# One 512-column subtraction on VectorE in place of two of 256, and a new list of order moves

## The chip, the core and the metric

The kernel runs on one core of a Trainium2 chip. The core has five engines that run side by side: TensorE (PE in the profile: matmuls; its weight loads are PEld), VectorE (DVE), ScalarE (ACT), GpSimd (POOL) and SyncE (SP), which here issues most of the DMAs that bring weights from HBM. They work on tiles of 128 partitions in SBUF; matmuls write to PSUM, in eight banks of 512 float32 columns. The metric is the device time of one execution in microseconds (us), lower is better. The kernel before took 1205.26 us, the median of three runs (1204.7, 1205.26, 1209.56).

## The reference

A decoder trunk of two layers, with 512 tokens and a model width of 1024, in float32. Layer 0 mixes causal pooling with an attention that keeps the 128 best-scored keys of each query; layer 1 is a gated linear recurrence. Each mixer is followed by a gated feed-forward network. Every block begins with an RMS norm and adds its result to `x`:

```python
def rmsnorm(x, g):
    xf = x.astype(jnp.float32)
    y = xf * lax.rsqrt(jnp.mean(xf * xf, axis=-1, keepdims=True) + EPS)
    return (y * g.astype(jnp.float32)).astype(x.dtype)

def swiglu(h, w_gate_up, w_down):
    gu = h @ w_gate_up
    gate, up = gu[..., :D_FF], gu[..., D_FF:]
    return (jax.nn.silu(gate) * up) @ w_down

for layer in range(DEPTH):
    h = rmsnorm(x, ln_mix[layer])
    ...                                   # layer 0: pooling and attention; layer 1: recurrence
    x = x + mixed @ w_out
    h = rmsnorm(x, ln_ffn[layer])
    x = x + swiglu(h, w_gate_up[layer], w_down[layer])
return rmsnorm(x, ln_final)
```

## The kernel before

**Data.** The residual `x` lies transposed in eight tiles `xT`, 128 model rows by 512 tokens each. A float32 product is made of three matmuls: weight and operand are each split into a high part, rounded to a faster float32 form, and a low correction. `wh`, `wl` are the two parts of 512 (or 384) weight columns; `BH[i]`, `BL[i]` those of an operand. ScalarE makes the high part by a copy, VectorE (for some GpSimd) subtracts it from the source to get the low one. Both `wh` and `wl` are rings of six buffers. Raw weights come into three buffers `raw`.

**Seven products for eight.** The input projections of the feed-forward networks and of layer 1 use a Strassen-like scheme on 2 by 2 blocks. The operand's halves by tokens are called here block one (tokens 0 to 255, z = 0) and block two (256 to 511, z = 1). For each i of 0 to 3, of model rows i and i + 4, the operand tiles `BH[i]` and `BL[i]` hold seven slots of 256 columns: B11, B21 (rows i and i + 4 of block one), B22 (row i + 4 of block two), and four sums. With y11, y21 the block-one rows and y12, y22 the block-two rows:

- T1 = y11 - y12, T3 = y22 - y12, T2 = y22 - T1, T4 = y21 - T2.

`pairs` (L837) first runs the products that need only B11 and B21 (`first`, `second`: 5 weight slabs before layer 1, 10 before a feed-forward network), which gives TensorE work while the sums are made. Then `rest` (L760) goes through S1 with T1, S2 with T2, S3 with T3, S4 with B22 and A22 with T4 for each slab.

**The bridges.** `Bridge` (L608) stands between two blocks. `add` and `add_half` add a product to `xT`, square it, and at the last tile of a token half run `norm` (column sums with the matrix `ones`, a square root, and a broadcast by matmuls with `idn`). `build` (L653) then makes the operands of that half. Three bridges use this `build`: r0 (before the feed-forward network of layer 0, around 205 us of the profile), r1 (before layer 1, around 560 us) and r2 (before the last feed-forward network, around 845 us). For z = 1 the kernel before has, per i, t3 on GpSimd and t1 on VectorE, each 256 columns, then t2 and t4 on VectorE. T1 and T2 lie in one page (`ta`), T3 and T4 in another (`tb`), so that one copy and one subtraction split a page. The low part of page `tb` is made by GpSimd for i = 1 and 3.

**Pages.** Temporary tiles of 512 columns come from a pool, first in, first out (18 pages from the first feed-forward network on). Who takes a page must wait until its last reader has finished.

**Order.** Nothing runs in the order of the code. `Plan` records every instruction with its operands and an estimated cost; `issue` (L400) schedules them by a list scheduler, and then applies each entry of `MOVES` (a seed, a strength, a start and a width of a stretch): it shakes the priorities in that stretch and keeps the order if the estimated end is earlier. The instructions are then issued in that order on each engine, and an engine's queue is strictly in order. All of them show one line in the profile (L425 before).

Of the kernel before, what the change touches and what calls it, by code (L numbers as in the profile page):

```python
# [15 lines left out]
ALU = mybir.AluOpType  # L16
AX = mybir.AxisListType

P = 128
T = 512  # L20
H2 = T // 2
# [19 lines left out]
ITERS = 6  # L41

MOVES = (
# [31 lines left out]
)  # L75
PAGES = 38
RPAGES = 20
# [10 lines left out]
TWO_PI_3 = float(np.float32(2 * np.pi - 6.28125 - 0.001953125))  # L88
MAGIC = 12582912.0

B11, B21, B22, T1, T2, T3, T4 = range(7)
OPND = {"A11": B11, "A12": B21, "A22": T4, "S2": T2, "S3": T3, "S1": T1, "S4": B22}

class Op:
# [334 lines left out]
def trunk(ctx: ExitStack, tc: tile.TileContext, xt, xp, pos, vecs, ident, dup, tri, lmask, invc, select,  # L429
          w_ab, w_kw, w_pool, w_oa, w_ob, w_c, w_oc, w_gu, w_dn, w_dq, out):  # L430
    nc = Plan(tc)
# [3 lines left out]
    def new(shape, dt, name):  # L435
        t = cp.tile(shape, dt, name=name)
        return t[tuple(slice(None) for _ in shape)]
# [33 lines left out]
    pages = Pool([new([P, T], F32, f"pg{i}") for i in range(PAGES - RPAGES)] + early_pg[NR:])  # L471
# [136 lines left out]
    class Bridge:  # L608
# [44 lines left out]
        def build(self, z, ts, rp):  # L653
            for i in range(4):
                bh, bl = BH[i], BL[i]
                pg = pages.get()
                ya, yb = pg[:, :H2], pg[:, H2:]
                for j, y in ((i, ya), (i + 4, yb)):
                    nc.vector.scalar_tensor_tensor(y, xT[j][:, ts], vec[:, self.gcol + j:self.gcol + j + 1], rp, ALU.mult, ALU.mult)
                if z == 0:  # L660
                    self.y[i] = pg
                    for s, y, e in ((B11, ya, nc.gpsimd), (B21, yb, nc.vector)):
                        h = bh[:, s * H2:(s + 1) * H2]
                        nc.scalar.activation(h, y, AF.Copy)
                        e.tensor_tensor(bl[:, s * H2:(s + 1) * H2], y, f32(h), ALU.subtract)
                else:
                    y11, y21 = self.y[i][:, :H2], self.y[i][:, H2:]
                    ta, tb = pages.get(), pages.get()
                    t1, t2, t3, t4 = ta[:, :H2], ta[:, H2:], tb[:, :H2], tb[:, H2:]
                    h = bh[:, B22 * H2:(B22 + 1) * H2]  # L670
                    nc.scalar.activation(h, yb, AF.Copy)
                    nc.gpsimd.tensor_sub(t3, yb, ya)
                    nc.vector.tensor_sub(t1, y11, ya)
                    nc.vector.scalar_tensor_tensor(t2, t1, -1.0, yb, ALU.mult, ALU.subtract)
                    nc.vector.scalar_tensor_tensor(t4, t2, -1.0, y21, ALU.mult, ALU.subtract)
                    h3, h1 = bh[:, 5 * H2:], bh[:, 3 * H2:5 * H2]
                    nc.scalar.activation(h3, tb, AF.Copy)
                    nc.scalar.activation(h1, ta, AF.Copy)
                    nc.vector.tensor_tensor(bl[:, B22 * H2:(B22 + 1) * H2], yb, f32(h), ALU.subtract)
                    (nc.gpsimd if i % 2 else nc.vector).tensor_tensor(bl[:, 5 * H2:], tb, f32(h3), ALU.subtract)  # L680
                    nc.vector.tensor_tensor(bl[:, 3 * H2:5 * H2], ta, f32(h1), ALU.subtract)
                    pages.put(self.y[i], ta, tb, pg)


    class Stage:
# [965 lines left out]
```

## Time and profile before

| | us |
|---|---|
| median of 3 runs | 1205.26 |
| the profiled execution | 1208.27 |
| span in its trace, first to last instruction | 1206.5 |
| PE busy | 1175.2 |
| DVE busy | 974.0 |
| ACT busy | 755.9 |
| POOL busy | 225.4 |

The profiled execution is 3.0 us longer than the median. PE is busy 97% of the span and DVE 81%. Busy shares are means over stages that differ: the rows further down show single stretches. The chain of work that ended last goes through PE for 76% of the span.

### The profile page before, as it was taken

How to read it: one execution, taken by the hardware profiler on the slowest of the kernel's cores; microseconds unless marked ns; L12 is line 12 of the kernel's file. 1: busy time of each engine (PE TensorE's matmuls, PEld its weight loads, DVE VectorE, ACT ScalarE, POOL GpSimd, SP SyncE). 2: the span in 40 equal slices, each digit the busy share in tenths (PEclk: the TensorE clock that was granted, in tenths of full speed). 3: DMA queues.
4: the chain of work that ended last, by engine and by line, in shares of the span. 5: the costliest groups of instructions: out<-in, count | busy, mean ns of one | idle time of the engine just before them, and what ended most of it. 6: DMA issues, size and time to landing. Idle time of an engine off the chain costs nothing.

```text
span 1206.5 us, 23123 instructions
## 1 busy us (share of the span) xinstructions
PE 1175.2 (97%) x8562; PEld 1077.9 (89%) x8563; DVE 974.0 (81%) x2116; ACT 755.9 (63%) x1753; POOL 225.4 (19%) x209
## 2 busy tenths in 40 slices
PE   8998999999999999998999999999999999999996
PEld 6776658999999988998999999988999999998996
DVE  7799966987777794778999999976987777795676
ACT  6336965766666762656877767744766566673563
POOL 4465012221101001102222211111221111000111
PEclk9997999999999999998999999999999999999999
DMA  8221113599877535467674445216599876634652
GB/s 314 102 70 53 36 39 84 187 235 237 233 182 190 127 110 148 130 160 202 196 190 118 125 119 143 71 53 158 163 233 243 219 183 167 169 97 129 150 151 70
DMA packets 72369, 180.60 MB, mean 150 GB/s; under 512 B 6144, under 2 KB 20544, under 8 KB 72256
## 3 DMA queue, kind: packets, MB, share of 16 engines
q1 hardware_dynamic: 51584, 141.37, 36.3%
q0 software_dynamic: 20672, 37.75, 18.9%
q8 instruction: 67, 1.10, 0.4%
q14 instruction: 46, 0.38, 0.1%
HBM read 177.00 MB, written 2.10 MB: 148 GB/s over the span
## 4 chain that ended last, share of the span: by engine, by line
PE 76%; DVE 6%; DMA 5%; ACT 2%; issue 1%; POOL 0%; DVEq 0%; ACTq 0%; POOLq 0%
PE bk L425 76%; DMA raw<-in_w_dq 3%; DVE wl L425 2%; DVE pg L425 2%; DMA raw<-in_w_gu 2%; ACT wh L425 1%; ACT pg L425 1%; DVE xT L425 1%; DVE raw L425 0%; DVE BL L425 0%; ACT bk L425 0%; ACT BH L425 0%; DVE sm L425 0%; DVE pr L425 0%; POOL pg L425 0%
## 5 line engine op out<-in xcount | busy, mean ns | idle before, releaser
L425 PE MATMUL bk<-BH,wh 128*128 128x256 f32 (+1 forms) x2088 | 581.7, 297 | 12.5 <-ACT wh L425 3.5
L425 PE MATMUL bk<-BL,wh 128*128 128x256 f32 (+1 forms) x2088 | 584.7, 294 | 0.0
L425 PE MATMUL bk<-BH,wl 128*128 128x256 f32 (+1 forms) x2088 | 576.6, 295 | 1.1 <-DVE wl L425 1.1
L425 ACT ACTIVATE wh<-raw 128x512 fp32r<-128x512 f32 (+2 forms) x644 | 378.4, 602 | 280.1 <-PE bk L425 229.0
L425 DVE TENSOR_TENSOR wl<-raw,wh 128x512 fp32r<-128x512 f32 (+1 forms) x609 | 397.0, 670 | 119.2 <-ACT wh L425 97.3
L425 PEld LDWEIGHTS bk<-BH,wh 128*128 128x128 f32 x2088 | 388.3, 192 | 29.4 <-ACT bk L425 6.3
L425 PEld LDWEIGHTS bk<-BL,wh 128*128 128x128 f32 x2088 | 391.6, 192 | 8.0 <-issue 0.8
L425 PEld LDWEIGHTS bk<-BH,wl 128*128 128x128 f32 x2088 | 387.4, 192 | 10.3 <-DVE wl L425 1.9
L425 PE MATMUL bk<-pr,wh 128*128 128x256 f32 (+1 forms) x784 | 190.3, 331 | 0.0
L425 PEld LDWEIGHTS bk<-pr,wh 128*128 128x128 f32 x784 | 132.1, 188 | 14.8 <-ACT wh L425 0.2
L425 PE MATMUL bk<-pr,wl 128*128 128x256 f32 (+1 forms) x392 | 128.6, 333 | 0.6 <-DVE wl L425 0.6
L425 DVE TENSOR_TENSOR raw<-raw 128x512 f32<-128x512 f32 (+1 forms) x152 | 100.8, 668 | 14.9 <-DMA raw<-in_w_gu 8.6
L425 POOL DMA_DIRECT2D raw<-in_w_gu x44 | 47.9, 1089 | 334.7 <-DVE wl L425 135.7
L425 DVE TENSOR_TENSOR pg<-pg,pg 128x256 f32<-128x256 f32 (+2 forms) x203 | 100.0, 504 | 8.8 <-ACT pg L425 4.0
L425 ACT COPY pg<-bk 128x256 f32<-128x256 f32 (+6 forms) x212 | 76.4, 365 | 33.8 <-PE bk L425 28.8
L425 ACT COPY bk<-bk 128x256 f32<-128x256 f32 x222 | 77.6, 362 | 20.5 <-PE bk L425 20.3
L425 PEld LDWEIGHTS bk<-pr,wl 128*128 128x128 f32 x392 | 73.4, 188 | 8.0 <-DVE wl L425 1.3
L425 PE MATMUL bk<-pg,pg 128*128 128x128 f32 (+3 forms) x578 | 69.0, 260 | 1.0 <-DVE pg L425 0.7
L425 PEld LDWEIGHTS bk<-pg,pg 128*128 128x128 f32 (+3 forms) x578 | 56.3, 167 | 8.1 <-ACT pg L425 2.1
L425 POOL TENSOR_TENSOR wl<-raw,wh 128x512 fp32r<-128x512 f32 (+3 forms) x35 | 45.5, 1303 | 94.2 <-ACT wh L425 86.9
L425 POOL TENSOR_TENSOR pg<-pg,pg 128x256 f32<-128x256 f32 (+1 forms) x36 | 38.1, 1058 | 132.1 <-ACT pg L425 59.0
L425 POOL DMA_DIRECT2D raw<-in_w_dq x16 | 17.5, 1102 | 216.3 <-DVE wl L425 103.9
(167 smaller groups left out, 1068.1 us busy)
## 6 DMA issues: line engine op xcount, KB each, us to landing
raw<-in_w_gu SPq DMA_DIRECT2D x44, 768.0 KB, 6.3
raw<-in_w_gu SPq DMA_DIRECT2D x64, 512.0 KB, 5.5
raw<-in_w_gu POOLq DMA_DIRECT2D x44, 512.0 KB, 6.3
raw<-in_w_c SPq DMA_DIRECT2D x16, 768.0 KB, 5.6
raw<-in_w_c SPq DMA_DIRECT2D x21, 512.0 KB, 4.2
raw<-in_w_dq SPq DMA_DIRECT2D x16, 576.0 KB, 5.4
raw<-in_w_c POOLq DMA_DIRECT2D x16, 512.0 KB, 5.6
raw<-in_w_dn SPq DMA_DIRECT2D x16, 448.0 KB, 3.4
```

The costliest lines, as they stand in the source:

```text
L425: getattr(self.real[o.eng], o.call)(*map(_real, o.args), **{k: _real(v) for k, v in o.kw.items()})
```

## The change

Block one now takes two pages per i, and each row of block two is written into the free half of one of them: page `pa` holds y11 and y22, page `pb` y12 and y21. Then `pa` less y12 taken twice is T1 and T3 in one VectorE instruction of 512 columns. The slots are renumbered so that T1 and T3 share a page and T2 and T4 the other. GpSimd's subtraction and VectorE's of 256 columns are gone. GpSimd still makes the low part of page `tb` for i = 1 and 3, which is now the one of T2 and T4. Each i takes four pages as before, two of them earlier. `MOVES` is another list, of 73 entries (92 before), so the order of instructions is new over the whole program.

```diff
 MOVES = (
-    (353236198, 1000, 372111, 20000), (664781755, 200, 1057486, 200000), (787263731, 2000, 158073, 40000),
+    (4522707, 2000, 934044, 40000), (491263128, 1000, 214385, 40000), (889732538, 2000, 362822, 40000),
...
-B11, B21, B22, T1, T2, T3, T4 = range(7)
+B11, B21, B22, T1, T3, T2, T4 = range(7)
...
-                pg = pages.get()
-                ya, yb = pg[:, :H2], pg[:, H2:]
+                if z == 0:
+                    self.y[i] = pages.get(), pages.get()
+                pa, pb = self.y[i]
+
+                ya, yb = (pa[:, :H2], pb[:, H2:]) if z == 0 else (pb[:, :H2], pa[:, H2:])
...
-                    t1, t2, t3, t4 = ta[:, :H2], ta[:, H2:], tb[:, :H2], tb[:, H2:]
+                    t1, t3, t2, t4 = ta[:, :H2], ta[:, H2:], tb[:, :H2], tb[:, H2:]
                     h = bh[:, B22 * H2:(B22 + 1) * H2]
                     nc.scalar.activation(h, yb, AF.Copy)
-                    nc.gpsimd.tensor_sub(t3, yb, ya)
-                    nc.vector.tensor_sub(t1, y11, ya)
+                    two = lambda x: x.rearrange("p (a b) -> p a b", a=2)
+                    nc.vector.tensor_tensor(two(ta), two(pa), ya[:, None, :].to_broadcast([P, 2, H2]), ALU.subtract)
                     nc.vector.scalar_tensor_tensor(t2, t1, -1.0, yb, ALU.mult, ALU.subtract)
...
-                    pages.put(self.y[i], ta, tb, pg)
+                    pages.put(pa, pb, ta, tb)
```

**VectorE at r1, block two.** Before, from the first row of block two on; `bk_150` is the broadcast norm of block two, `pg_141` the page of T1 and T2, `pg_127` that of T3 and T4, both of i = 0:

```order
L425 SCALAR_TENSOR_TENSOR pg_133<-xT_65,vec,bk_150 128x256
L425 SCALAR_TENSOR_TENSOR pg_133<-xT_69,vec,bk_150 128x256
L425 TENSOR_TENSOR pg_141<-pg_134,pg_133 128x256
L425 SCALAR_TENSOR_TENSOR pg_130<-xT_70,vec,bk_150 128x256
L425 SCALAR_TENSOR_TENSOR pg_141<-pg_141,pg_133 128x256
L425 TENSOR_TENSOR wl_92<-raw_81,wh_86 128x512
L425 TENSOR_TENSOR wl_95<-raw_81,wh_89 128x512
L425 SCALAR_TENSOR_TENSOR pg_127<-pg_141,pg_134 128x256
L425 SCALAR_TENSOR_TENSOR pg_130<-xT_66,vec,bk_150 128x256
L425 TENSOR_TENSOR wl_94<-raw_82,wh_88 128x512
L425 TENSOR_TENSOR BL_77<-pg_127,BH_73 128x512
```

Now, from the same row on; `pg_142` and `pg_132` are the two pages of i = 0, `pg_139` is T1 and T3, `pg_133` T2 and T4:

```order
L419 SCALAR_TENSOR_TENSOR pg_132<-xT_65,vec,bk_150 128x256
L419 SCALAR_TENSOR_TENSOR pg_142<-xT_69,vec,bk_150 128x256
L419 SCALAR_TENSOR_TENSOR pg_138<-xT_66,vec,bk_150 128x256
L419 TENSOR_TENSOR pg_139<-pg_142,pg_132 128x512
L419 SCALAR_TENSOR_TENSOR pg_135<-xT_70,vec,bk_150 128x256
L419 SCALAR_TENSOR_TENSOR pg_133<-pg_139,pg_142 128x256
L419 TENSOR_TENSOR pg_130<-pg_135,pg_138 128x512
L419 TENSOR_TENSOR BL_77<-pg_139,BH_73 128x512
L419 SCALAR_TENSOR_TENSOR pg_133<-pg_133,pg_132 128x256
```

The subtraction is 512 wide, the first page that is split is that of T1 and T3, and the corrections of weights that stood among these rows stand elsewhere.

**PE just before r1.** The last product of the layer 0 network into bank `bk_143` is nine rows of `BH`, three of `BL` and six matmuls with `pr`, 18 in all, and the column sums with `ones` belong to the two norms (`bk_150` block one, `bk_149` block two). Before, the 18 stand ahead of all of these rows:

```order
L425 MATMUL bk_143<-pr_3414,wl_93 128x256
L425 MATMUL bk_150<-ones,pg_125 128x1
L425 MATMUL bk_150<-ones,pg_128 128x1
...
L425 MATMUL bk_149<-ones,pg_137 128x1
L425 MATMUL bk_148<-idn,sm_98 128x128 x2
L425 MATMUL bk_146<-BH_73,wh_88 128x256
```

Now they stand between the two norms:

```order
L419 MATMUL bk_150<-ones,pg_126 128x1
L419 MATMUL bk_143<-BH_73,wh_86 128x256
L419 MATMUL bk_143<-BL_77,wh_86 128x256
...
L419 MATMUL bk_143<-pr_3475,wl_93 128x256
L419 MATMUL bk_149<-ones,pg_125 128x1
L419 MATMUL bk_148<-idn,sm_98 128x128 x2
```

The sums of block one no longer wait in PE's queue for the 18 matmuls.

**GpSimd at r1.** Before, `pg_127`, `pg_129`, `pg_136` and `pg_137` are written with T3, between the corrections of the operands:

```order
L425 TENSOR_TENSOR BL_79<-pg_140,BH_75 128x256
L425 TENSOR_TENSOR pg_127<-pg_133 128x256
L425 TENSOR_TENSOR pg_129<-pg_130 128x256
L425 TENSOR_TENSOR BL_78<-pg_129,BH_74 128x512
L425 TENSOR_TENSOR pg_136<-pg_142 128x256
L425 TENSOR_TENSOR pg_137<-pg_128 128x256
L425 TENSOR_TENSOR BL_80<-pg_137,BH_76 128x512
```

Now these four rows are gone, and the two corrections of 512 columns are of T2 and T4:

```order
L419 TENSOR_TENSOR BL_79<-pg_131,BH_75 128x256
L419 TENSOR_TENSOR BL_80<-pg_127,BH_76 128x256
L419 TENSOR_TENSOR BL_78<-pg_136,BH_74 128x512
L419 TENSOR_TENSOR BL_80<-pg_141,BH_76 128x512
L419 DMA raw_82<-in_w_c 128x2x512
```

GpSimd has 12 instructions less in the whole program, four at each bridge.

## Rows read from the trace of the kernel before

**Rows 1.** The page's first part: busy us, share of span, count.
```profile
PE 1175.2 (97%) x8562; PEld 1077.9 (89%) x8563; DVE 974.0 (81%) x2116; ACT 755.9 (63%) x1753; POOL 225.4 (19%) x209
```

**Rows 2.** Stretches at r0, r1, r2: stretch, length, busy by engine, clock, DMA share, GB/s.
```profile
215.00:245.00 30.00, 29.87 (x247) 29.48 (x246) 29.13 (x53) 24.65 (x57) 8.66 (x7) 1.00 0.64 193
...
555.00:590.00 35.00, 30.56 (x215) 29.55 (x215) 34.10 (x72) 24.47 (x57) 11.46 (x12) 0.85 0.65 188
...
849.00:880.00 31.00, 30.50 (x252) 30.11 (x252) 30.32 (x54) 24.52 (x56) 7.03 (x6) 1.00 0.57 185
```

**Rows 3.** Timeline of PE at r1: start, us, instruction, count, [idle before, releaser].
```profile
555.79 1.22 PE L425 MATMUL bk<-idn,sm 128*128 128x128 f32 x4 [0.32 <-DVE sm L425]
558.04 0.58 PE L425 MATMUL bk<-BH,wh 128*128 128x256 f32 x1 [1.03 <-ACT BH L425]
...
560.83 0.41 PE L425 MATMUL bk<-BH,wh 128*128 128x256 f32 x1
561.04 0.46 PE L425 MATMUL bk<-BL,wh 128*128 128x256 f32 x1
...
566.22 0.58 PE L425 MATMUL bk<-BH,wh 128*128 128x256 f32 x1 [2.58 <-ACT pg L425]
...
581.28 0.38 PE L425 MATMUL bk<-idb 128*128 128x512 bf16 x1
...
586.23 0.50 PE L425 MATMUL bk<-BH,wh 128*128 128x256 f32 x2 [0.51 <-ACT bk L425]
```

**Rows 4.** Timeline of ACT at r1.
```profile
565.79 0.37 ACT L425 COPY pg<-bk 128x256 f32<-128x256 f32 x1 [1.49 <-DVE BL L425]
```

**Rows 5.** Timeline of DVE at r1.
```profile
554.50 0.16 DVE L425 TENSOR_SCALAR sm<-bk 128x2 f32<-128x2 f32 x1 [0.36 <-PE bk L425]
...
557.06 0.48 DVE L425 SCALAR_TENSOR_TENSOR pg<-xT,vec,bk 128x256 f32<-128x256 f32 x1
...
557.99 2.44 DVE L425 SCALAR_TENSOR_TENSOR pg<-xT,vec,bk 128x256 f32<-128x256 f32 x6
560.34 0.82 DVE L425 TENSOR_TENSOR pg<-pg,pg 128x256 f32<-128x256 f32 x1
...
564.49 1.21 DVE L425 TENSOR_TENSOR BL<-pg,BH 128x512 fp32r<-128x512 f32 x1
...
574.97 1.45 DVE L425 TENSOR_TENSOR pg<-pg,pg 128x256 f32<-128x256 f32 x2
...
585.77 1.89 DVE L425 TENSOR_TENSOR wl<-raw,wh 128x512 fp32r<-128x512 f32 x3
587.57 1.09 DVE L425 TENSOR_TENSOR BL<-pg,BH 128x256 fp32r<-128x256 f32 x3
```

**Rows 6.** Timeline of POOL at r1.
```profile
560.84 0.92 POOL L425 TENSOR_TENSOR pg<-pg 128x256 f32<-128x256 f32 x1
564.05 1.11 POOL L425 TENSOR_TENSOR pg<-pg 128x256 f32<-128x256 f32 x1 [2.29 <-DVE pg L425]
...
574.14 2.00 POOL L425 TENSOR_TENSOR pg<-pg 128x256 f32<-128x256 f32 x2 [4.28 <-DVE pg L425]
582.41 1.68 POOL L425 TENSOR_TENSOR BL<-pg,BH 128x512 fp32r<-128x512 f32 x1 [6.27 <-ACT BH L425]
```

**Rows 7.** Groups by form: shapes, count, busy us, mean ns, idle before.
```profile
L425 POOL TENSOR_TENSOR pg<-pg 128x256 f32<-128x256 f32 x10 | 10.3, 1034 | 28.2 <-DVE pg L425 28.2
...
L425 POOL TENSOR_TENSOR BL<-pg,BH 128x512 fp32r<-128x512 f32 x5 | 8.2, 1633 | 20.6 <-ACT BH L425 17.3 <-DVE pg L425 3.3
...
L425 DVE TENSOR_TENSOR pg<-bk,idn 128x512 f32<-128x512 f32 x8 | 5.4, 679 | 0.0
```

**Rows 8.** Timeline of DVE, PE and POOL at r2.
```profile
851.43 1.23 DVE L425 TENSOR_TENSOR wl<-raw,wh 128x512 fp32r<-128x512 f32 x1
...
852.73 0.39 PE L425 MATMUL bk<-BH,wl 128*128 128x256 f32 x1 [0.34 <-DVE wl L425]
...
851.33 0.79 POOL L425 TENSOR_TENSOR pg<-pg 128x256 f32<-128x256 f32 x1 [4.43 <-DVE pg L425]
```

More of the change, by code (lines that the diff above doesn't have):

```diff
@@ L660, in build @@
                 if z == 0:
-                    self.y[i] = pg
                     for s, y, e in ((B11, ya, nc.gpsimd), (B21, yb, nc.vector)):
@@ L666, in build @@
                 else:
-                    y11, y21 = self.y[i][:, :H2], self.y[i][:, H2:]
+                    y21 = pb[:, H2:]
                     ta, tb = pages.get(), pages.get()
-                    t1, t2, t3, t4 = ta[:, :H2], ta[:, H2:], tb[:, :H2], tb[:, H2:]
+                    t1, t3, t2, t4 = ta[:, :H2], ta[:, H2:], tb[:, :H2], tb[:, H2:]
                     h = bh[:, B22 * H2:(B22 + 1) * H2]
                     nc.scalar.activation(h, yb, AF.Copy)
-                    nc.gpsimd.tensor_sub(t3, yb, ya)
-                    nc.vector.tensor_sub(t1, y11, ya)
+                    two = lambda x: x.rearrange("p (a b) -> p a b", a=2)
+                    nc.vector.tensor_tensor(two(ta), two(pa), ya[:, None, :].to_broadcast([P, 2, H2]), ALU.subtract)
                     nc.vector.scalar_tensor_tensor(t2, t1, -1.0, yb, ALU.mult, ALU.subtract)
```

54 rows, old and new, of the table MOVES are left out of this document.

## The prediction

> **What bounds the kernel now.** I read the page's first part first, because it says how much any change could win: PE is busy 1175.2 us of a span of 1206.5, so it stands idle 31.3 us in the whole program [rows 1]. The change takes no matmul away. What it can give is a part of these 31.3 us, or of time that PE runs at its lower clock. The windows around the three bridges come second, to see which engine leads in each [rows 2]. At r0 PE is busy 29.87 of 30 us and at r2 30.50 of 31, both at a granted clock of 1.00, while DVE is busy 29.13 and 30.32: DVE is nearly full there, but PE does not wait for it. At r1 it does: PE is busy 30.56 of 35 us, the clock is 0.85, and DVE is busy 34.10. So r1 is the place to take apart, and PE's timeline there comes third [rows 3]. Its marked waits are 0.32, 1.03, 2.58 and 0.51 us, 4.44 together. After the first of them matmuls of 128x256 start 0.21 us apart (560.83, 561.04), where at full clock one takes 29.87/247 = 0.121 us [rows 2, 3].
>
> The 2.58 us wait ends at a copy by ACT of a finished product into a page. That copy waited 1.49 us for a correction of an operand on DVE [rows 4], the one of 512 columns at 564.49 that ends at 565.70 and with it lets its page go [rows 5]. So the longest wait at r1 is one for a page, which the rows of block two on DVE, between the norm and the first correction, hold back. The change rewrites exactly these rows.
>
> **The change part by part.**
>
> *GpSimd loses 12 subtractions* of 256 columns, four at a bridge: ten rows have a mean of 1.034 us [rows 7], so about 12.4 us go. GpSimd is busy 225.4 us of the span [rows 1] and waits 28.2 us for DVE ahead of these ten [rows 7]: by itself this is worth nothing.
>
> *VectorE has 512 columns in place of 256, 12 times.* Three corrections of 256 columns take 1.09 us and three of 512 take 1.89 undisturbed [rows 5], so a step is about 0.34 and 0.605 us, as a bound from the other side 0.679 for the one form in the trace that reads a broadcast operand [rows 7]. The difference is 0.27 (0.34 at most), 3.2 us for 12 (4.1).
>
> *VectorE no longer runs beside GpSimd's T3.* Where they meet at r1, DVE's rows are long: 0.82 us for 256 columns at 560.34 beside GpSimd's 560.84, 1.21 for 512 at 564.49 beside 564.05, and 1.45 for two of 256 at 574.97 beside 574.14 [rows 5, 6]. By themselves they would be 0.41 (0.48 for six of the others is 2.44/6 = 0.41), 0.68 and 0.75. The sum of the stretches is 0.41 + 0.53 + 0.70 = 1.64 us for four T3, 0.41 each; at r2 it is 0.55, where a correction of weights takes 1.23 [rows 8]. By 0.41, 12 of them give 4.9 us back. DVE's net is 3.2 - 4.9 = -1.7 us, some -0.57 at each bridge; between bounds of +4.1 (nothing given back) and -3.4 (0.55 each). At r0 and r2 PE hides nearly all of it: it is idle 0.13 us of 30 and 0.50 of 31 [rows 2].
>
> A rule of the Trainium skill speaks for a larger gain: the page "SBUF — State Buffer", section "SBUF: two separate sides", says that VectorE and GpSimd share a port pair under an exclusive lock, so that the loser stands for the whole of the other's instruction. By the rule the 12.4 us of GpSimd's rows would come back on DVE whole, and its net would be -9.2 us. The traced stretches are 0.41 us beside rows of 1.03, less than half of it, so here the rule holds in direction and not in size, and the sum goes by 0.41.
>
> *r1, the page that PE waits for.* Before, from the first row of block two on DVE to the release of the page is 565.70 - 557.06 = 8.64 us [rows 5]. After, the row that lets go is the correction of T1 and T3 further down DVE's queue. Up to it I count 12 rows of the norm's scaling or of T2 and T4 at 0.39 to 0.41, two subtractions of 512 at 0.605, five rows of 256 at 0.34 and one correction of 512, about 8.6 us. The chain to the page is as long as it was. The start of block two moves by two things. From the norm's small row at 554.50 it took 2.56 us to the first row of block two [rows 5]. Now four rows of 256 columns (0.34 each), four corrections of 512 (0.605 each) and about 0.8 us of small rows stand there, 4.6 us: +2.0. And 18 products that PE had ahead of block one's sums now stand behind them, so that block one starts 18 x 0.121 = 2.2 us earlier [rows 2]. Net -0.2 us: nothing that I can tell from the order. The bounds are +1.8 (the 18 save nothing, since PE is already ahead) and -4.44 (all waits of the four rows go) with a clock that never falls. What a full clock would give: 247 matmuls take 29.87 us, at the 0.85 of r1 the 35 us lose 0.15 x 35 = 5.25 [rows 2].
>
> *r1, what comes later.* T1 is wanted 95 matmuls after the first product (121 before), so the earlier use eats what the wide instruction saves. T2 and T4 for the odd i are corrected on GpSimd, 1.68 us at 582.41 [rows 6] against 0.605 on DVE. By the pace of before the first use of the last of these falls where PE was at about 582 (581.28 is close by [rows 3]), and the count of rows puts the end of GpSimd's correction some 2 us ahead. I take it as hidden, with 2.1 us (584.09 - 582) if it stands where it did.
>
> *r2.* PE waits 0.34 us at 852.73 for DVE's correction of weights, which takes 1.23 us beside GpSimd's T3 at 851.33, in place of 0.68 [rows 8]. That wait goes: -0.34.
>
> *The rest of the order* is new in every stage, with the same matmuls, the same DMAs and as many pages. PE had 31.3 us idle [rows 1], of which 4.44 at r1; the other 27 lie mostly at the start, at the top-k and at the tail, where the queues read nearly alike. A new order can gain or lose single waits of 0.3 to 2.6 us like those of [rows 3]; four of them with random signs come to about 4 us either way. I take 0.
>
> Sum: -0.2 - 0.34 = -0.54. The profiled execution took 1208.27, its span 1206.5 and 1.8 us around it, and it would become 1207.7. The median of the runs is 1205.26, 3.0 less than this execution, so the forecast goes from the median: 1204.7 us.
>
> **The rivals.**
>
> *A, the stall at r1 goes altogether.* Block one's norm is reached before the 18 products, DVE is nowhere held up by GpSimd, the page comes free while PE is still fed, and the clock stays at its upper level. That gives 4.44 + 5.25 = 9.7, so about 1195.6 us. For it: the longest wait is behind DVE, and one of the rows in that chain is stretched from 0.68 to 1.21. Against: the counted chain is as long as before, and more rows stand ahead of its start. The rule of the skill above would help this rival: 9.2 us of DVE time, a third of it at r1, is 3.1 us and more than the 2.58 us wait. Chance 0.15.
>
> *B, slower: GpSimd's share is now on the path.* The page that GpSimd corrects holds T2 and T4, the last links of the chain, and no longer T3 and T4; T2 is used ahead of T3. GpSimd takes 1.63 us for 512 columns [rows 7] where DVE takes 0.605, and starts only when T4 is made and copied. If PE reaches T2 of the odd i before that, it stands for the difference. At r1 that is 2.1 us, and as much at r0 and r2 by the same difference: 6.3, about 1211.5. If the clock falls with it as it does now with 4.44 us of waits, 2.1/4.44 x 5.25 = 2.5 us more, 8.8 in all and about 1214 us. It decides if GpSimd's correction for i = 3 ends more than 2 us later than I count. For it: GpSimd waits 6.27 us for ACT's copy before that very row [rows 6]. Against: 143 matmuls stand between the first product and the first use of it. Chance 0.12.
>
> *C, the instruction isn't worth what it says.* With a broadcast operand 512 columns could cost two of 256 or more. Against: 0.679 us for such a form [rows 7], though that one reads PSUM. At 1.0 us in place of 0.605 it would cost 12 x 0.4 = 4.7 us of DVE, of which r1 pays 1.6: about 1207. Chance 0.03.
>
> **How the numbers follow.** The forecast has 0.70, A 0.15, B 0.12, C 0.03. A measurement of this kernel can tell about 0.5% from no change, 6.0 us: below 1199.2 is faster, above 1211.3 slower. The forecast's own range is 1200 to 1209, from the 4 us of the new order and from +1.8 at r1. A lies with nearly all its weight in faster, with 0.04 from the forecast's lower edge: 0.19. B lies in slower with most of its weight, and 0.03 come from the forecast's upper edge: 0.14. For 8 in 10 the range reaches over the nearer part of A and up to B without its clock: 1197.5 to 1211.5.
>
> **What would show it.** Right: DVE's rows of 512 columns that write a page at the bridges take 0.55 to 0.7 us; DVE has no row of 256 columns above 0.6 there; POOL's busy time falls by 11 to 13 us and DVE's by 1 to 3; at r1 PE still waits 1 to 3 us for ACT's copy of a product, and the clock of the stretch is 0.8 to 0.9. A is right if PE's marked waits at r1 sum to under 1 us and the clock there is above 0.95. B is right if PE's rows behind the first product show a wait that ends at a POOL correction of 512 columns. C is right if the wide rows take 0.9 us or more. The forecast is wrong, whatever the time, if PE's idle time changes by over 4 us at a place other than the three bridges: then the list of moves made the time, and the rewritten step did not.

## The result, and the profile after

The changed kernel takes 1213.55 us, the median of 8 runs (1210.24 to 1216.48); the kernel before took 1205.03 us in 8 runs (1201.45 to 1209.56). The ratio is 1.0051, with a 95% interval of 1.0027 to 1.0075. So it is slower, by about 0.5%, and its time lies 2 us above the upper end of the predicted range. In the profiled execution of 1210.99 us the span is 1209.2 us. The page's first part, beside [rows 1]:

```profile
PE 1172.3 (97%) x8562; PEld 1076.0 (89%) x8563; DVE 973.3 (80%) x2116; ACT 755.5 (62%) x1753; POOL 220.2 (18%) x197
```

PE has the same matmuls and is idle for 1209.2 - 1172.3 = 36.9 us, 5.6 more than before. GpSimd has the 12 instructions less, but is only 5.2 us less busy. The stretches at r0, r1 (45 us here) and r2, beside [rows 2]:

```profile
215.00:245.00 30.00, 29.62 (x246) 29.40 (x245) 29.73 (x57) 24.34 (x56) 4.58 (x3) 1.00 0.59 201
555.00:600.00 45.00, 38.88 (x262) 36.52 (x262) 38.29 (x89) 30.13 (x68) 13.47 (x9) 0.85 0.62 178
849.00:880.00 31.00, 30.40 (x244) 29.42 (x243) 29.14 (x63) 24.02 (x57) 7.97 (x5) 1.00 0.49 165
```

At r0 and r2 PE is full as before. What PE waits for at r1, beside [rows 3]:

```profile
555.45 0.38 PE L419 MATMUL bk<-BH,wh 128*128 128x256 f32 x1 [1.42 <-DVE xT L419]
...
558.78 0.58 PE L419 MATMUL bk<-ones,pg 128*128 128x1 f32 x2 [0.34 <-DVE pg L419]
559.52 1.23 PE L419 MATMUL bk<-idn,sm 128*128 128x128 f32 x4 [0.16 <-DVE sm L419]
560.90 1.44 PE L419 MATMUL bk<-ones,pg 128*128 128x1 f32 x6 [0.15 <-ACT pg L419]
562.67 0.80 PE L419 MATMUL bk<-BH,wh 128*128 128x256 f32 x2 [0.33 <-ACT BH L419]
...
571.17 0.58 PE L419 MATMUL bk<-BH,wh 128*128 128x256 f32 x1 [2.54 <-ACT pg L419]
...
588.50 0.39 PE L419 MATMUL bk<-BL,wh 128*128 128x256 f32 x1 [1.77 <-POOL BL L419]
...
589.88 0.39 PE L419 MATMUL bk<-BH,wh 128*128 128x256 f32 x1 [0.28 <-ACT bk L419]
```

Together 6.99 us, where it was 4.44. The wait for the page is as long as ever, 2.54 against 2.58. New are the first, 1.42 us ahead of the 18 products that now stand between the two norms, and the one for GpSimd at 588.50. Behind the second stands this row of GpSimd, beside [rows 6]:

```profile
575.87 1.29 POOL L419 TENSOR_TENSOR BL<-pg,BH 128x512 fp32r<-128x512 f32 x1 [10.28 <-ACT BH L419]
582.71 5.74 POOL L419 TENSOR_TENSOR BL<-pg,BH 128x512 fp32r<-128x512 f32 x1 [5.55 <-ACT BH L419]
```

One correction of 512 columns takes 1.29 us and the next, of the same form, 5.74. In the groups by form this row now has six instructions, 16.0 us busy. Before, they were five with 8.2 us [rows 7] and a sixth of 1.6 us under another tile name, 9.8 together. These 6.2 us more are most of what is missing between the 12.4 us that the 12 subtractions took and the 5.2 us that GpSimd saves. After, and the sixth of before:

```profile
L419 POOL TENSOR_TENSOR BL<-pg,BH 128x512 fp32r<-128x512 f32 x6 | 16.0, 2668 | 58.0 <-ACT BH L419 58.0
```

```profile
L425 POOL TENSOR_TENSOR BL<-pa,BH 128x512 fp32r<-128x512 f32 x1 | 1.6, 1556 | 7.5 <-ACT BH L425 7.5
```

Last, why block two comes late at r1. ScalarE and VectorE between the sums of block one and its broadcast:

```profile
556.96 0.63 ACT L419 ACTIVATE wh<-raw 128x512 fp32r<-128x512 f32 x1 [3.10 <-DMA raw<-in_w_c]
557.50 0.19 ACT L419 ACTIVATE sm<-sm 128x2 f32<-128x2 f32 x1
```

```profile
555.31 0.16 DVE L419 RECIPROCAL sm<-sm 128x2 f32<-128x2 f32 x1
557.62 0.69 DVE L419 TENSOR_TENSOR wl<-raw,wh 128x512 fp32r<-128x512 f32 x1 [2.16 <-ACT wh L419]
558.23 0.15 DVE L419 TENSOR_TENSOR sm<-sm 128x2 f32<-128x2 f32 x1
```

The reciprocal is done at 555.47, but ScalarE's square root (`sm<-sm`) stands in its queue behind a split of weights whose transfer is 3.10 us late, and VectorE's next rows stand behind the correction of the same weights. Block two's last sums come at 560.90. In the kernel before, the sums of both blocks came in one row of 16 matmuls, and block two's broadcast followed at 558.42:

```profile
553.52 1.96 PE L425 MATMUL bk<-ones,pg 128*128 128x1 f32 x16
...
558.42 1.05 PE L425 MATMUL bk<-idn,sm 128*128 128x128 f32 x4
```

### The profile page after: what moved, and what is told of

The parts are those of the page before. It is cut to its first block, busy times and chain, and to the rows that moved or that the text cites. A ratio compares the mean times of both kernels' runs of the same rounds, so it can differ in the third digit from the quotient of the medians.

```text
span 1209.2 us, 23102 instructions
## 1 busy us (share of the span) xinstructions
PE 1172.3 (97%) x8562; PEld 1076.0 (89%) x8563; DVE 973.3 (80%) x2116; ACT 755.5 (62%) x1753; POOL 220.2 (18%) x197
## 4 chain that ended last, share of the span: by engine, by line
PE 79%; DVE 7%; ACT 5%; DMA 4%; issue 2%; POOL 1%; SPq 0%; DVEq 0%; ACTq 0%; POOLq 0%
PE bk L419 79%; DVE pg L419 2%; DMA raw<-in_w_gu 2%; DVE wl L419 2%; ACT pg L419 2%; ACT wh L419 2%; DMA raw<-in_w_dq 1%; DVE sm L419 1%; ACT BH L419 1%; DMA raw<-in_w_c 1%; DVE BL L419 1%; DMA xT<-in_xt 1%; DVE raw L419 1%; POOL BL L419 0%; SPq L419 0%
## 5 line engine op out<-in xcount | busy, mean ns | idle before, releaser
L419 DVE TENSOR_TENSOR pg<-pg,pg 128x256 f32<-128x256 f32 (+2 forms) x203 | 103.5, 520 | 8.1 <-ACT pg L419 3.9
L419 DVE SCALAR_TENSOR_TENSOR pg<-bk,pg 128x256 f32<-128x256 f32 x110 | 46.0, 418 | 14.3 <-PE bk L419 12.0
```

Source lines behind the costliest of these rows:

```text
L419: getattr(self.real[o.eng], o.call)(*map(_real, o.args), **{k: _real(v) for k, v in o.kw.items()})
```

## The experiments

Each group ran on one chip together with the kernel before; the chips differ by some 4 us (medians of the kernel before from 1205.0 to 1209.4), so only ratios are compared. Two theories were there from the start. **S**: the rewritten step costs the time, through what it does to the queues at the bridges. **O**: the new order over the whole program costs it, whatever the step. In all kernels but the two without a list and the last two, the search is replaced by a list `KEY` of the planned starts, by which `issue` sorts, with the dependencies kept:

```diff
     def issue(self):
-        best = None
...
-        run(list(range(n)), ITERS)
-        for seed, sigma, a, w in MOVES:
...
+        h = [(KEY[i], i) for i in range(n) if not left[i]]
+        heapq.heapify(h)
+        while h:
+            i = heapq.heappop(h)[1]
+            order.append(i)
...
```

### The two kernels again

`c_after` and `c_before` have each kernel's own order in that form.

> The changed kernel, with its own order given as a list in place of the search (the same instructions in the same order). Both theories: 1.005 to 1.009 times the kernel before on the same chip. It says how much of the last four runs is the chip.

> The kernel before with its own order given as a list. Both theories: 0.998 to 1.002 times the kernel before. Its profile is a second one of the kernel before: the stretch from 504 to 554 us should again take 49 to 51 us if the list decides it, and up to 54 if the transfers of that run do.

Measured: c_after 1.0048 (1.0029 to 1.0068), c_before 0.9997 (0.9976 to 1.0019). The loss is there again, and writing the order as a list changes nothing that these runs resolve. The profiles of this pair are 9.4 us apart (spans 1215.4 and 1206.0). Two stretches, of c_before and then of c_after, show most of it:

```profile
500.00:552.00 52.00, 50.31 (x415) 49.44 (x414) 38.62 (x84) 30.16 (x67) 4.38 (x4) 1.00 0.65 170
552.00:592.00 40.00, 34.11 (x263) 32.95 (x263) 38.67 (x84) 28.18 (x63) 13.20 (x13) 0.96 0.70 197
```

```profile
500.00:552.00 52.00, 48.39 (x396) 47.31 (x395) 36.79 (x79) 27.89 (x64) 4.61 (x5) 1.00 0.64 157
552.00:592.00 40.00, 31.86 (x212) 30.32 (x210) 32.51 (x77) 23.53 (x55) 12.01 (x8) 0.83 0.61 176
```

PE's idle time grows from 1.69 to 3.61 us ahead of r1 and from 5.89 to 8.14 at r1, and the clock's loss at r1 from 0.04 x 40 = 1.6 to 6.8 us. In the first pair of profiles (before and after) the same two stretches gain only 0.54 and 2.57 us of idle time, and the clock's loss at r1 goes from 5.2 to 6.8. The mean clock of the whole run does not tell the kernels apart: over its nine runs c_after had 0.988, the kernel before 0.986 beside it.

PE's idle time over the whole span is 36.9 and 37.9 us in two profiles of the changed order, 31.3 and 35.0 in two of the old one. So the two of the old order lie 3.7 us apart, and in the second pair idle time is 2.9 of the 9.4 us; the rest is in PE's busy time (1171.0 and 1177.5 us), for the same matmuls, and about as large as the 5.2 us by which the clock's loss at r1 grows.

PE runs the same matmuls in all four (8562 by the page; one more is recorded in the c_ kernels), so a profile can be cut where a given number of them has begun. Time in us of four parts; the third holds r1 (about 543 to 648 us):

| profile | matmuls to 2700 | to 3500 | to 4300 | the rest |
|---|---|---|---|---|
| before | 422.7 | 119.8 | 105.0 | 559.1 |
| after | 424.4 | 120.4 | 107.6 | 556.8 |
| c_before | 423.4 | 119.2 | 104.5 | 558.9 |
| c_after | 424.8 | 121.9 | 110.7 | 557.9 |

The part with r1 loses 2.6 us in the first pair and 6.2 in the second. All the rest together loses 0.1 and 3.2 us.

### One order in the other program, and splices of the two

`e1_after_before_order` is the changed program sorted by the starts of the kernel before, `e2_before_after_order` the reverse; in `g1_after_with_before_ff0` and `g2_before_with_after_ff0` only the instructions between r0 and r1 are sorted by the other kernel's starts. In the four, from instruction 1600 on in the e kernels and 1700 in the g kernels, a page is taken by the earliest last use, so that the other order fits. That changes which instructions wait for a page as well. The edit in e1:

```diff
         def get(self):
-            return self.free.pop(0)
+            if len(nc.ops) < 1600 or _psum(self.free[0]):
+                return self.free.pop(0)
+            last = lambda b: max([KEY[r[4].i] for r in nc.acc.get(b.tensor.name, [])], default=0)
+            return self.free.pop(min(range(len(self.free)), key=lambda k: last(self.free[k])))
```

> The changed kernel with the instructions in the order of the kernel before, given as a list (in block two the second scaling row of each i and the rows of T4 are moved up next to their neighbours, since the wide row and the page of T2 and T4 need them). Theory S (the step): the loss comes from the rewritten rows themselves, above all from GpSimd's correction of T2 and T4, which takes 5.74 us at r1 in the profile after and lets PE wait 1.77 us. Then this kernel is slow as well: 1210 us or more. Theory O (the order): the loss of about 8 us comes from the new list of moves, in waits spread over the program. Then it is 1203 to 1207 us.

> The kernel before with the instructions in the order of the changed kernel, given as a list; GpSimd's T3 stands where the wide row stands. Theory S: without the new rows it is near the kernel before, 1207 us or less. Theory O: the order alone costs the time, 1210 to 1214 us.

> The changed kernel, where the instructions between r0 and r1 alone (about 250 to 550 us, no rewritten row among them) stand in the order of the kernel before. Theory O: the new list loses 3 to 5 us in this stretch, so that 3 to 5 us come back and the ratio to the kernel before is 1.002 to 1.004. Theory S: nothing comes back, 1.005 to 1.008.

> The kernel before, where the instructions between r0 and r1 alone stand in the order of the changed kernel. Theory O: 3 to 5 us more than the kernel before, ratio 1.0025 to 1.004. Theory S: no more than 1 us, ratio 0.999 to 1.001.

Measured: e1 1.0080 (1.0057 to 1.0102), e2 1.0153 (1.0127 to 1.0179), g1 1.0041 (1.0026 to 1.0057), g2 1.0114 (1.0091 to 1.0136). e1, 1219.5 us, meets what S had said of it (1210 us or more); e2, with the new order in the old program, is far above what S had said and above O's range too; g1's interval reaches into the ranges of both; g2 is above both. The old order does not save the changed program, and the new order makes the old program slower than the changed one. g1 should have taken the idle time ahead of r1 back, and did not: PE waits there for weights again. PE and ScalarE in g1:

```profile
507.38 0.58 PE L515 MATMUL bk<-BH,wh 128*128 128x256 f32 x1 [2.76 <-ACT wh L515]
```

```profile
506.39 1.76 ACT L515 ACTIVATE wh<-raw 128x384 fp32r<-128x384 f32 x4 [3.95 <-DMA raw<-in_w_dq]
```

Against each program with its own order (1.0048 for c_after, 0.9997 for c_before), e1 costs about 0.3%, g1 nothing, e2 1.5% and g2 1.1%. So the old program pays for the foreign order, the changed one little or nothing. Since the other way to take pages differs from both kernels too, the four don't tell S from O.

### Parts of the step at the bridges

`e3_tb_on_vector` gives GpSimd's corrections of T2 and T4 to VectorE; `e4_two_narrow` takes the wide row apart again.

```diff
-                    (nc.gpsimd if i % 2 else nc.vector).tensor_tensor(bl[:, 5 * H2:], tb, f32(h3), ALU.subtract)
+                    nc.vector.tensor_tensor(bl[:, 5 * H2:], tb, f32(h3), ALU.subtract)
```

```diff
-                    nc.vector.tensor_tensor(two(ta), two(pa), ya[:, None, :].to_broadcast([P, 2, H2]), ALU.subtract)
+                    nc.gpsimd.tensor_sub(t3, yb, ya)
+                    nc.vector.tensor_sub(t1, pa[:, :H2], ya)
```

> The changed kernel in its own order; only the low part of the page of T2 and T4 for i = 1 and 3 is made by VectorE and no longer by GpSimd (6 instructions). Theory S: the wait of 1.77 us at r1 goes and the clock there rises, 3 to 5 us less than the changed kernel, 1208.5 to 1210.5 us. Theory O: only the marked wait goes, 1 to 2 us, 1211.5 to 1212.5 us.

> The changed kernel in its own order, where the wide subtraction is again two of 256 columns, T3 on GpSimd and T1 on VectorE, with the new pages. Both theories: the wide row is not what costs the time, so 1212 to 1215 us, within 1.5 us of the changed kernel. If the wide row itself is dear, it is 1209 us or less.

Measured: e3 1.0090 (1.0069 to 1.0111), e4 1.0084 (1.0059 to 1.0109). Neither gives anything back; both lie above c_after's 1.0048, and e4, expected within 1.5 us of the changed kernel, is some 4 us above it by the ratios. In e3 GpSimd's wait is gone, and PE waits elsewhere:

```profile
576.45 0.39 PE L515 MATMUL bk<-BH,wh 128*128 128x256 f32 x1 [1.85 <-ACT pg L515]
...
618.50 1.22 PE L515 MATMUL bk<-pg,pg 128*128 128x128 f32 x4 [3.58 <-DVE pg L515]
```

The second is a late transfer: VectorE had waited for it at 617.42. f2, below, has the same wait (3.79 us), and no profile of the changed kernel in its own order has it (after, c_after, f1). So the two kernels that take the corrections off GpSimd win 1.8 us at one place and lose 3.6 to 3.8 at another, and don't show what the time would be without GpSimd's correction alone.

```profile
617.42 0.69 DVE L515 TENSOR_TENSOR raw<-raw 128x512 f32<-128x512 f32 x1 [3.50 <-DMA raw<-in_w_c]
```

In e4, where GpSimd has T3 back, PE still waits for GpSimd's correction, so the wide row is not what this wait needs:

```profile
591.52 0.39 PE L515 MATMUL bk<-BL,wh 128*128 128x256 f32 x1 [2.03 <-POOL BL L515]
```

Two more aimed at r1 alone. `f1_norm_first` moves 15 rows of the changed order: the square root and the small rows of block one's norm ahead of the late weights' splits, and the first scaling rows ahead of three corrections. `f2_norm_first_vector` also gives the two corrections of T2 and T4 at r1 to VectorE.

In the list of f1, 43 rows have another place than in c_after's, among places 5543 to 5592. Row 5456 goes from 5547 to 5544 and row 5540 from 5549 to 5545; 5457, 5458 and 5459 go from 5558, 5564 and 5573 to 5547 to 5549, and 5541 from 5560 to 5551; 5460 and 5461 go from 5578 and 5579 to 5574 and 5575, and 5468, 5463 and 5462 from 5583, 5587 and 5592 to 5578 to 5580. Most of the others move down to make room. f2 has the same list, and takes these two corrections alone from GpSimd.

> The changed kernel in its own order, but for 15 rows at r1: the square root and the small rows of block one's norm no longer stand behind the splits of the first w_c weights on ScalarE and VectorE, which wait 3.1 to 3.5 us for their transfer in the profiles of the changed kernel. Theory N (norm behind late weights): the four matmuls with idn follow block one's sums some 2 us earlier, PE's idle time at r1 falls by 2 to 4 us, and the ratio to the kernel before falls from 1.005 to 1.002 or 1.003. Theory G (GpSimd's correction of T2 and T4): the wait of 1.8 us for GpSimd stays and grows by what is won ahead of it, so that the ratio stays at 1.004 or more.

> As f1_norm_first, and at r1 VectorE makes the low parts of T2 and T4 for i = 1 and 3, no longer GpSimd (two instructions). Theory G: 2 to 3 us less than f1_norm_first, the PE wait behind GpSimd gone. Theory N: no more than 1 us less than f1_norm_first, since VectorE takes on 1.2 us.

Measured: f1 1.0047 (1.0024 to 1.0069), f2 1.0056 (1.0029 to 1.0083). PE at r1 in f1:

```profile
558.80 0.61 PE L515 MATMUL bk<-idn,sm 128*128 128x128 f32 x4
561.01 0.83 PE L515 MATMUL bk<-ones,pg 128*128 128x1 f32 x6 [1.50 <-ACT pg L515]
...
563.49 0.58 PE L515 MATMUL bk<-BL,wh 128*128 128x256 f32 x1 [1.05 <-POOL BL L515]
...
572.67 0.58 PE L515 MATMUL bk<-BH,wh 128*128 128x256 f32 x1 [1.52 <-ACT pg L515]
...
590.22 0.39 PE L515 MATMUL bk<-BL,wh 128*128 128x256 f32 x1 [1.78 <-POOL BL L515]
```

The norm comes at once and the wait for the page is a microsecond shorter, as theory N said. But block two's sums wait 1.50 us for ScalarE's square, GpSimd's corrections of block one are late by 1.05, and the last wait is what it was. The waits only move: their sum at r1 is 8.25 us, against 6.99 in the profile after and 8.77 in c_after, and the ratio is not the 1.002 to 1.003 that theory N had named.

### The same treatment for both programs

The last way to tell S from O gives both programs lists of the same kind. `n_after_plain` and `n_before_plain` have none; the four `l_` kernels have lists from new searches with the planner's own rules, some 95,000 tries each from the empty list, two for each program.

```diff
-MOVES = (
-    (4522707, 2000, 934044, 40000), (491263128, 1000, 214385, 40000), (889732538, 2000, 362822, 40000),
...
+MOVES = ()
```

> The changed kernel with an empty list of moves, so that the planner's first order stands. Theory S (the step itself costs): 4 to 10 us slower than the same of the kernel before (n_before_plain). Theory O (the list costs): within 3 us of it, or faster.

> The kernel before with an empty list of moves. Theory S: 4 to 10 us faster than n_after_plain. Theory O: within 3 us of it, or slower. Both: slower than the kernel before by 10 to 40 us, which says what a list of moves is worth.

> The changed kernel with another list of moves, from a search of its own of some 95,000 tries with the planner of the kernel, which starts from the empty list as the next three do. Theory S (the step costs): both kernels with the step are slower than both without it by 4 us or more. Theory O (the list decides): the two lists of one program lie as far apart as lists of the two programs do, 4 us or more, and the programs don't separate; the step's own share is between -6 and +2 us.

> The changed kernel with a second list from such a search. Theory S: within 3 us of l_after_1, and 4 us or more slower than l_before_1 and l_before_2. Theory O: it can be 4 us or more away from l_after_1, on either side of the kernels without the step.

> The kernel before with another list from such a search. Theory S: faster than l_after_1 and l_after_2 by 4 us or more. Theory O: as slow as these, since its list is of the same kind: 1.005 to 1.02 times the kernel before.

> The kernel before with a second list from such a search. Theory S: as l_before_1. Theory O: 4 us or more from l_before_1, or as slow as the changed kernel with its searched lists.

| list | with the step | without it |
|---|---|---|
| as given | 1.0051 (1.0027 to 1.0075) | 1 |
| none | 1.0207 (1.0162 to 1.0252) | 1.0241 (1.0201 to 1.0281) |
| first search | 1.0138 (1.0105 to 1.0171) | 1.0109 (1.0087 to 1.0131) |
| second search | 1.0070 (1.0041 to 1.0098) | 1.0028 (1.0009 to 1.0047) |

Without a list the program with the step is the faster one, 1234.5 against 1240.2 us, though the intervals overlap. Two searches that differ in their random numbers alone lie 0.68% apart with the step and 0.81% without it, some 8 to 10 us, which is more than the whole effect of the change. In total time the programs don't separate, as theory O said. What the step does by itself is not resolved: the four rows give +0.5, -0.3, +0.3 and +0.4%, and two lists of one program differ by more than any of these.

Cut by matmuls as above, the part with r1 shows more, though it was looked at only afterwards and in one profile each. With own lists it takes, in us:

| list | with the step | without it |
|---|---|---|
| as given | 107.6, 110.7 | 105.0, 104.5 |
| none | 113.9 | 109.4 |
| first search | 109.3 | 106.9 |
| second search | 111.9 | 105.5 |

It is slower with the step in each row, by 2.4 to 6.4 us. So a cost of the step at r1, whatever the list, is a rival that these runs leave standing. Against it, e2 and g2, which lack the step, take 111.2 and 111.9 us there under a foreign order.

### VectorE and GpSimd side by side

The last two kernels leave the whole computation out and run rows of VectorE beside one of GpSimd.

```diff
+        for k in range(n):
+            nc.vector.tensor_tensor(dv[k % 4], go if k == 0 else x[k % 4], x[4 + k % 4], ALU.subtract)
+        nc.gpsimd.tensor_tensor(gp, g2, x[0], ALU.subtract)
+        nc.vector.tensor_tensor(jn, gp, dv[(n - 1) % 4], ALU.add)
```

> A kernel of its own that computes nothing of the reference: ScalarE writes two tiles, which start an unbroken row of n subtractions of 512 columns on VectorE (both operands in SBUF) and, 0.6 us later, one subtraction on GpSimd; each case twice: n = 0, 2, 4, 8, 12 with 512 columns on GpSimd, n = 8 with 256, and n = 8 with an operand of VectorE in PSUM. Theory G (GpSimd is held until VectorE pauses): its row takes about 1.3 us alone and 1.3 us more than what is left of VectorE's row, some 2, 3, 5.5 and 8 us for n = 2, 4, 8, 12, and 1.3 to 2 us with PSUM. Rival (they take turns, one of VectorE's for one of GpSimd's): 1.3 to 2 us for every n, and one VectorE row stretched by 0.4 to 1.3 us.

> As m1_port, a kernel of its own that computes nothing of the reference. VectorE's row is 8 subtractions of 512 columns each time, and GpSimd's subtraction of 512 columns becomes ready at 15 different moments of it: ScalarE's copy that it waits for has 64 to 512 columns, or is one of 512 and one of 64 to 448. In m1_port GpSimd asked 0.05 us ahead of a VectorE row's start and had its turn at once, in 1.26 us. Theory G2 (it depends on the moment): asked in the middle of a VectorE row GpSimd waits until VectorE pauses and ends up to 4 us later, 5 us in all; asked at the border of two rows it has its turn, so that both kinds are seen among the 15. Rival (turns): 1.26 to 1.9 us in all 15, VectorE's row 1.1 us longer in each.

GpSimd and VectorE in m1_port with n = 8, then with 256 columns on GpSimd, then with an operand of VectorE in PSUM:

```profile
30.25 1.26 POOL L32 TENSOR_TENSOR gp<-g,x 128x512 f32<-128x512 f32 x1 [3.81 <-ACT g L28]
30.30 5.38 DVE L31 TENSOR_TENSOR dv<-x,x 128x512 f32<-128x512 f32 x7
...
65.38 0.72 POOL L32 TENSOR_TENSOR gp<-g,x 128x256 f32<-128x256 f32 x1 [8.62 <-ACT g L28]
65.42 4.84 DVE L31 TENSOR_TENSOR dv<-x,x 128x512 f32<-128x512 f32 x7
...
79.26 1.27 POOL L32 TENSOR_TENSOR gp<-g,x 128x512 f32<-128x512 f32 x1 [6.21 <-ACT g L28]
79.30 4.27 DVE L31 TENSOR_TENSOR dv<-bk,x 128x512 f32<-128x512 f32 x7
```

Seven rows by themselves take six steps of 0.602 us and a last row of 0.69, 4.3 us; with an operand in PSUM they take 4.27 beside GpSimd. Beside 512 columns on GpSimd they take 5.38, beside 256 they take 4.84. So GpSimd had its turn at once, and VectorE stood for about 1.09 us (beside 1.26) and 0.55 (beside 0.72). In m2_port_phase the moment was moved; one of its cases, in GpSimd's and VectorE's rows:

```profile
14.16 1.57 POOL L30 TENSOR_TENSOR gp<-g,x 128x512 f32<-128x512 f32 x1 [7.92 <-ACT g L27]
```

```profile
14.53 5.36 DVE L29 TENSOR_TENSOR dv<-x,x 128x512 f32<-128x512 f32 x7
```

1.57 us is the longest of the 15. The first of them (1.26 us) had no row of VectorE beside it; in the other 14 GpSimd waits for the end of the VectorE row that is under way and is next. Theories G and G2 fall for these rows, and with them the plain explanation of the 5.74 us.

## Why the prediction was wrong

**The wide row** was right: 0.60 us from its start to the next (568.10 to 568.70), costed at 0.605.

```profile
566.92 1.26 DVE L419 SCALAR_TENSOR_TENSOR pg<-xT,vec,bk 128x256 f32<-128x256 f32 x3
568.10 0.68 DVE L419 TENSOR_TENSOR pg<-pg,pg 128x512 f32<-128x512 f32 x1
568.70 0.47 DVE L419 SCALAR_TENSOR_TENSOR pg<-xT,vec,bk 128x256 f32<-128x256 f32 x1
...
570.03 0.68 DVE L419 TENSOR_TENSOR BL<-pg,BH 128x512 fp32r<-128x512 f32 x1
```

**VectorE's net** of -1.7 us: its busy time fell by 0.7 (974.0 to 973.3), and by 1.3 in the second pair of profiles (974.7 to 973.4). The sign was right, the gain smaller than forecast. The bench gives a longer stretch than 0.41 us: 0.55 beside 256 columns of GpSimd. The Trainium skill's rule in "SBUF — State Buffer", section "SBUF: two separate sides", that the loser stands for the whole of the other's instruction, fits the bench in size to within 0.17 us (1.09 of 1.26, 0.55 of 0.72). The kernel does not bear it out: by 0.55 each the net would have been 3.2 - 6.6 = -3.4, by the whole of GpSimd's rows -9.2, and both are further from the measured fall than the -1.7 by 0.41. At r0 and r2 it made no difference, since PE hid it as forecast.

**r1, the page** is the main step that failed: "The start of block two moves by two things", with "Net -0.2 us". The row at 557.06 that the prediction calls block two's first is block one's: block two's broadcast matmuls start only at 558.42. So its two terms are those of block one's start, and the chain to the release goes from block one's first row. Block one's first row comes at 560.92 in place of 557.06, 3.9 us later and not 0.2 earlier. The rows that I counted ahead of it are there, but between them VectorE waits 2.16 us for a split of weights whose transfer is 3.10 us late, so the way from the norm's small row is 6.34 us (554.58 to 560.92) where I had 4.6. And the 18 products gave nothing back: block one's sums start 0.44 us earlier (553.08), its small row 0.08 later. I had named this as the bound of +1.8, but not the late weights.

The chain from block one's first row to the release then takes 570.71 - 560.92 = 9.79 us, where I had counted 8.6. The reason is the start of block two: its last sums come 7.4 us later (560.90 against 553.52), and its own first row too (566.92, by the order of its rows 559.55 before). From that row to the release it is 3.79 us now, eight rows, and was 6.15, so the wide row and the new order did shorten this part. The page is released 5.0 us later in all. PE's wait for it is as long as before (2.54 against 2.58) only because PE comes 5.0 us later as well. That the wait stayed, as forecast, was luck.

By the matmuls, the part with r1 takes 2.6 us more in the first pair and 6.2 in the second, where the prediction had -0.2. That shows where time was lost. That the late norm is what loses it is argued from the profiles and not shown: f1 took the norm out from behind the late weights, and the waits came up elsewhere.

**r1, what comes later** failed too: "I take it as hidden". GpSimd's correction for i = 3 was late, as rival B said, by 1.77 us where the rival had 2.1; its other places, r0 and r2, show no such wait. B had the mechanism at one bridge out of three, and 1.8 us of its 8.8. Its 1214 us, close to the measured time, is then luck in size. What the kernel would take without this correction is not shown, since e3 and f2 bring a new wait of 3.6 to 3.8 us with it.

**r2**: the 0.34 us wait went, as forecast.

**The rest of the order**, "I take 0" with some 4 us either way, came to +0.1 and +3.2 us in the two pairs of profiles, so it is not what failed. But the width was small by what the lists show: two lists of the same planner lie 8 to 10 us apart in the same program, and every other list that was tried was slower than the old one. My own sign of failure, idle time that changes by over 4 us away from the bridges, is not met: ahead of r1 it grew by 0.5 and 1.9 us, and nowhere else by more than 3.0 (from 100 to 200 us, in the first pair alone). Of the signs of being right, the wide row, the wait for ACT's copy and the clock of 0.85 came; GpSimd's busy time fell by 5.2 us and not by 11 to 13, VectorE's by 0.7 and not by 1 to 3.

Rival A did not come, its clock neither: PE's waits at r1 sum to 6.99 us. Rival C is refuted by the wide row.

**What stays open**: the cause. The cuts by matmuls put most of the loss of the two pairs at r1, but not whether the step or the list makes it there, and no single row that was moved took it back. The step's share of the whole time lies between about -1 and +1%, an estimate from the spread of the lists.

## What to carry to other kernels

Where a change comes with a new searched order, measure both programs under several lists before the step is judged, and give the forecast the spread of the lists: here two lists of one program lie 0.7 to 0.8% apart, and the change was 0.5%. A search fits the order to estimated durations; what it can't see, here weights that arrive 3 us late, then stands at the head of an in-order queue with the norm behind it. One wait of the right size is no proof of a sum: look at the length and at the start of the chain behind it, and check which half or tile the first row of that chain belongs to. Where two kernels run the same matmuls, cut their profiles at the same matmul: it shows where time is lost, which idle time alone does not.

## What was not expected of the hardware

GpSimd's last correction at r1 ends late: it takes 5.74 us in the profile after, in c_after and in f1_norm_first alike. In the profile after it ends at 588.45, 1.26 us (a whole row in the bench) after 587.19. VectorE's rows follow each other without a pause from 577.34 on. The one at 582.70 is under way when GpSimd asks, the one at 586.91 is the last, and it ends at 587.33, 3.09 us ahead of the next:

```profile
582.70 0.68 DVE L419 TENSOR_TENSOR BL<-pg,BH 128x512 fp32r<-128x512 f32 x1
...
586.91 0.42 DVE L419 TENSOR_TENSOR BL<-pg,BH 128x256 fp32r<-128x256 f32 x1
590.42 1.48 DVE L419 TENSOR_TENSOR wl<-raw,wh 128x512 fp32r<-128x512 f32 x2 [3.09 <-ACT wh L419]
```

It looks as if GpSimd had its turn only when VectorE paused. But that is not general. In the bench GpSimd had its turn behind the row under way each time, and so it had in the kernel before, where its row at 582.41 took 1.68 us [rows 6] and VectorE's next row stood for it, 1.69 us in place of 0.68:

```profile
582.95 1.69 DVE L425 TENSOR_TENSOR BL<-pg,BH 128x512 fp32r<-128x512 f32 x1
```

What makes the difference (rounded outputs, waits on other engines in VectorE's rows, or something else) was not tried.
